# A hybrid S5 and RG-LRU layer on one core: one more product between splits and their users, four S5 runs at once, and a reordered tail

## The chip, the cores and the metric

One core of a Trainium2 chip runs the whole kernel. The metric is device time in microseconds, the median of repeated runs. Engines are named as in the profile: PE is TensorE (matmuls), DVE is VectorE, ACT is ScalarE, POOL is GpSimd, SP is SyncE, which here only issues transfers; POOL issues transfers too.

## The reference, cut to what matters

`x` is 2048 prompt frames and 8 x 16 sample frames of width 1024.

```
h = rmsnorm(x, ln_g);  u_a, z_a, u_b, z_b, g_a, g_b = split(h @ w_in)   # 512 512 1024 1024 1024 1024
y_a = gelu(s5(u_a));  y_a = y_a * sigmoid(y_a @ w_glu + b_glu)
p_a = (y_a * silu(z_a)) @ w_pa
y_b = rglru(conv4(u_b));  p_b = (y_b * silu(z_b)) @ w_pb
m = sigmoid(g_a) * p_a + sigmoid(g_b) * p_b
y = rmsnorm(x + m @ w_out, final_gain)
```

The S5 branch has 32 groups of 16 channels and 64 complex states each, the RG-LRU has 16 heads with block-diagonal gates. The states after the last frame are outputs too. All in float32.

## The kernel before, in words

**Numbers.** Every float32 operand is split into a float16 high part (an ACT copy) and a float16 low part (a DVE subtraction), and a product of two such operands is three passes (high-high, high-low, low-high), the lines 161 to 163 of the listing. A product with 4 blocks of the contracted axis is 12 matmuls of 128x128 by 128x512.

**Tiles.** Time is cut into four prompt tiles of 512 columns (n = 0 to 3) and one sample tile of 128 (n = 4).

**Stages.** (1) For each tile: norm, transposes of `x` into `h`, and the projection `u_a` (`proj`, four products m of 24 matmuls). `trans_tile(n+1, ...)` transposes the next tile behind the products m = 2 and m = 3, four channel blocks behind each; a transpose goes to one of the three buffers of the PSUM tag "a", which ACT and DVE empty (`evac_h`). `norm_sums`, `norm_root` and `norm_scale` for the next tile are written behind the products m = 0 and m = 1. (2) Four column blocks of `g_b` directly. (3) Sixteen pairs of column blocks (`run_pair`), alternating a pair of branch B (`u_b`, `z_b`) and a pair of gates; each pair is two times 7 products (a Strassen-like scheme, 12 matmuls each) and one of the sample tile. (4) The projection of branch B (`wpb`), 5 tiles by 8 blocks; called B below. (5) The tail: for each tile GLU and projection of branch A (`ga_tile`, 4 + 8 products), the output projection and final norm (`out_tile`). In the tail `glu_prep` loads the S5 output `ya` and splits it into `yh`, the first operand of the GLU.

**The order of the work.** All is one program written out in order; each engine runs its own instructions in that order. Beside the products of (2), (3) and (4) generators are advanced by `pump(budget)`, called once behind each product of 12 matmuls (each half product in B, each product of the sample tile): this is a turn. A generator that yields a number or `Step(c)` has put instructions of about c units in the program, and c is taken from the turn's budget; `Step` also ends its part of the turn, and `Later(k)` makes it sit out k turns. The list `tasks` is served first, the list `low` from what is left. In `tasks` are `b_work` (conv, gates and scan of branch B) and, in B, the 16 `s5_run(q)`; in `low` are `w_spill` (44 weight blocks split and stored) and two `s5_prep` (the 16 S5 matrices; the second works only in B).

An `s5_prep` of one q: load parameters, `Later(3)` or in B `Later(6)`, `wb` (five DVE operations, 2.2 units), transposes of `wb` (line 172 on PE, 0.8), `wc` (2.8), matmuls with `wc` (lines 1269 and 1272, 0.9), 0.7, then `kh` is stored to `kpD` and read back shifted as `dd` (0.4). What becomes of `dd`, `lags(q)`, is written during the next q of the same generator: two ACT copies and a store to `sD`; only then is q in `prepared`.

An `s5_run` of one q:

```python
            while q not in prepared or running > 2:
                yield Later(1)
            running += 1
            page = page_b("t1", (2048,), "sp", F32)
```

then it loads `sD[q]` and the inputs, `yield Later(7)`, and has the steps 0.6 (12 matmuls, line 1425), 3.4 (the DVE scan), 0.3, 0.8, 0.6, 0.6, 0.6 (two groups of matmuls, lines 1470 to 1477, whose results are stored to `yDp`). The pages "t1" have four buffers.

Behind B, what is left in the lists is worked off without products, then the tail starts:

```python
        while tasks or low or due:
            beside()
        load_w(wpa, wpaD[1])
```

`gt` tiles come from `slots` buffers, `small` tiles from `NSMALL`. `NO_SPILL` and `NO_PREP` are the turns of two neighbouring pairs (1 to 30) in which `w_spill` and `s5_prep` stand still.

## Time and profile before

| | |
|---|---|
| median of 3 runs | 1581.39 us (1579.0 to 1585.59) |
| the profiled execution | 1582.97 us, its span 1581.2 us |
| PE busy | 1456.8 us (92%), 8168 matmuls |
| DVE, ACT, POOL busy | 1038.7, 813.8, 275.1 us |
| mean granted clock of PE | 0.976 |

The granted clock is 1.0 at 2.4 GHz and 0.5 at 1.2 GHz. Idle time of PE is what a change of the order can win; idle time of another engine costs nothing unless PE waits for it. A matmul of 512 columns starts 0.216 us after the one before it at the full clock, though its own row says 0.38 us, since they overlap: a product of 12 is 2.6 us.

### The profile page before, as it was taken

What the parts mean: (1) busy time and instruction counts of PE and PEld (TensorE: products, weight loads), DVE (VectorE), ACT (ScalarE), POOL (GpSimd) and SP (SyncE); (2) the same over time, 40 slices, a digit from 0 to 9 for tenths busy, and PEclk for the clock granted to TensorE, in tenths of its full rate; (3) what the DMA queues carried; (4) which work ended last, traced back from release to release, by engine and by line L of the source; (5) the groups of instructions that cost most, each with busy time, mean ns of one, the idle gap of its engine ahead of it and who ended that gap; (6) DMA issues with size and microseconds to landing.
All of it is one profiled execution on the core that took longest, in us unless ns stands there. A gap on an engine that the chain in (4) does not pass through costs nothing.

```text
span 1581.2 us, 22662 instructions
## 1 busy us (share of the span) xinstructions
PE 1456.8 (92%) x8168; PEld 727.6 (46%) x8168; DVE 1038.7 (66%) x2137; ACT 813.8 (51%) x1524; POOL 275.1 (17%) x557
## 2 busy tenths in 40 slices
PE   7889999989999999999999999899998789999998
PEld 4444444444444444444444444455556334444444
DVE  5456867858677576877858777456545665757554
ACT  7542335847667575775847576234323432525232
POOL 0680010110201112020111202134324000000000
PEclk9999999999999999999999999999999799999999
DMA  8316222342422334142232408998973914352431
GB/s 203 91 54 247 71 76 78 106 125 70 144 61 96 102 103 134 48 155 64 94 104 77 152 22 296 318 294 287 311 248 105 345 74 148 118 178 89 166 99 69
DMA packets 168490, 222.20 MB, mean 141 GB/s; under 512 B 39259, under 2 KB 117739, under 8 KB 166329
## 3 DMA queue, kind: packets, MB, share of 16 engines
q1 hardware_dynamic: 144440, 150.96, 29.8%
q0 software_dynamic: 23936, 69.79, 12.2%
q8 instruction: 64, 1.05, 0.3%
q14 instruction: 50, 0.40, 0.1%
HBM read 133.85 MB, written 86.84 MB: 140 GB/s over the span
## 4 chain that ended last, share of the span: by engine, by line
PE 55%; DVE 19%; issue 12%; ACT 7%; DMA 4%; POOL 2%; SPq 1%; DVEq 0%; POOLq 0%; ACTq 0%
PE ps_mm L162 14%; PE ps_mm L161 14%; PE ps_mm L163 14%; PE ps_mm L1753 3%; PE ps_mm L1751 3%; PE ps_mm L1752 3%; DVE xc L65 3%; DVE wf L65 2%; DVE yh L53 2%; ACT L74 1%; PE ps_a L1272 1%; ACT pt L74 1%; DVE sz L65 1%; DVE wc L53 1%; DVE q L65 1%
## 5 line engine op out<-in xcount | busy, mean ns | idle before, releaser
L161 PE MATMUL ps_mm<-T,wf 128*128 128x512 f16 x512 | 195.4, 382 | 4.8 <-ACT ub L74 3.7
L163 PE MATMUL ps_mm<-T,wf 128*128 128x512 f16 x512 | 195.4, 382 | 0.5 <-DVE wf L65 0.5
L162 PE MATMUL ps_mm<-T,wf 128*128 128x512 f16 x512 | 195.4, 382 | 0.0
L161 PEld LDWEIGHTS <-wf 128*128 128x128 f16 x1232 | 121.5, 99 | 119.7 <-issue 9.5
L162 PEld LDWEIGHTS <-wf 128*128 128x128 f16 x1232 | 121.5, 99 | 118.6 <-issue 11.7
L163 PEld LDWEIGHTS <-wf 128*128 128x128 f16 x1232 | 121.5, 99 | 118.1 <-issue 5.1
L161 PE MATMUL ps_mm<-h,wf 128*128 128x512 f16 x448 | 173.2, 387 | 2.0 <-ACT wf L74 2.0
L163 PE MATMUL ps_mm<-h,wf 128*128 128x512 f16 x448 | 172.5, 385 | 0.7 <-DVE wf L65 0.7
L162 PE MATMUL ps_mm<-h,wf 128*128 128x512 f16 x448 | 172.9, 386 | 0.0
L1753 PE MATMUL ps_mm<-wo,M 128*128 128x512 f16 (+2 forms) x280 | 104.5, 375 | 5.3 <-DVE M L65 5.3
L1751 PE MATMUL ps_mm<-wo,M 128*128 128x512 f16 (+2 forms) x280 | 104.3, 374 | 0.0
L1752 PE MATMUL ps_mm<-wo,M 128*128 128x512 f16 (+2 forms) x280 | 104.3, 374 | 0.0
L161 PE MATMUL ps_mm<-Y,wpb 128*128 128x512 f16 x256 | 97.8, 382 | 0.4 <-DMA Y<-ybD 0.4
L162 PE MATMUL ps_mm<-Y,wpb 128*128 128x512 f16 x256 | 97.8, 382 | 0.0
L163 PE MATMUL ps_mm<-Y,wpb 128*128 128x512 f16 x256 | 97.6, 381 | 0.0
L65 DVE SCALAR_TENSOR_TENSOR gb<-gb,ps_mm 128x512 f32<-128x512 f32 (+1 forms) x40 | 24.1, 606 | 92.2 <-PE ps_mm L163 74.7
L74 ACT ACT_TABLE_LOAD x62 | 79.5, 1283 | 6.2 <-PE ps_mm L163 4.6
L65 DVE SCALAR_TENSOR_TENSOR xc<-ub,PC,xc 128x512 f32<-128x512 f32 x96 | 71.9, 749 | 2.3
L65 DVE SCALAR_TENSOR_TENSOR xo<-ps_mm,xo 128x512 f32<-128x512 f32 (+2 forms) x35 | 23.7, 676 | 72.5 <-PE ps_mm L1753 72.5
L74 ACT ACTIVATE gs<-ps_mm 128x512 f32<-128x512 f32 (+1 forms) x92 | 48.1, 532 | 44.8 <-PE ps_mm L163 39.3
L65 DVE SCALAR_TENSOR_TENSOR wf<-wraw,wf 128x512 f16<-128x512 f32 (+1 forms) x82 | 55.7, 696 | 12.0 <-ACT wf L74 12.0
L162 PE MATMUL ps_mm<-yA,wt 128*128 128x512 f16 (+1 forms) x160 | 54.2, 347 | 9.8 <-DVE yA L65 9.8
(318 smaller groups left out, 3254.5 us busy)
## 6 DMA issues: line engine op xcount, KB each, us to landing
wraw<-w_in SPq DMA_DIRECT2D x38, 512.0 KB, 4.0
sp<-sD SPq DMA_DIRECT2D x16, 768.0 KB, 7.7
xt<-x_prompt SPq DMA_DIRECT2D x16, 512.0 KB, 4.3
gbD<-gs POOLq DMA_DIRECT2D x32, 256.0 KB, 2.4
ybD<-y POOLq DMA_DIRECT2D x32, 256.0 KB, 3.3
gaD<-gs POOLq DMA_DIRECT2D x32, 256.0 KB, 2.4
Y<-ybD SPq DMA_DIRECT2D x8, 1024.0 KB, 13.8
gb<-gbD SPq DMA_DIRECT2D x32, 256.0 KB, 8.2
```

Of the source, the lines that this page charges most:

```text
L53: V.tensor_tensor(out=out, in0=a, in1=b, op=op)
L65: V.scalar_tensor_tensor(out=out, in0=a, scalar=s, in1=b, op0=op0, op1=op1)
L74: S.activation(out=out, in_=a, func=f, **kw)
L161: PE.matmul(p, lhsT=a[:, 0], rhs=b[:, 0], start=first, stop=False, skip_group_check=more)
L162: PE.matmul(p, lhsT=a[:, 0], rhs=b[:, 1], start=False, stop=False, skip_group_check=more)
L163: PE.matmul(p, lhsT=a[:, 1], rhs=b[:, 0], start=False, stop=last, skip_group_check=more)
L1272: PE.matmul(o[:, 16 + P * j:16 + P * j + w], lhsT=lb, rhs=wc[:, j, g].rearrange("p (h t) -> p t h", t=8)[:, 0:w // 16], start=True, stop=True)
L1751: PE.matmul(p, lhsT=lh[0], rhs=w_[:, 0, c], start=(k == 0), stop=False)
L1752: PE.matmul(p, lhsT=lh[0], rhs=w_[:, 1, c], start=False, stop=False)
L1753: PE.matmul(p, lhsT=lh[1], rhs=w_[:, 0, c], start=False, stop=(k == KB - 1))
```

## The change

- **Transposes.** For tiles 0 to 2 and m = 2, 3 two of the four transposed channel blocks are written in the middle of the product m (behind its fourth block), two behind it.
- **Turns.** `pump` carries what a turn overspent into the next (`debt`, down to -4). The budgets are 2.8 instead of 2.4 in the pairs and 2.5 instead of 2.2 in B.
- **One more product.** `b_work` has an empty stage between `xs_lo` and `gates`; `s5_prep` has a `Later(1)` behind `wb` and one behind `wc`. `kf` and `kh` share a buffer.
- **Windows and buffers.** `NO_SPILL`, `NO_PREP` move; 22 and 9 buffers instead of 21 and 12.
- **S5 runs.** Four at once instead of three, their earliest starts three turns apart instead of four.
- **The start of the tail.** A new task, `tail_start`, waits until all other tasks are done, then loads `wo` (4 x 1 MB) and runs `glu_prep(0)`; this was behind B before.
- **The tail.** Tiles in the order 0, 1, 4, 2, 3; what runs beside which `out_tile` is a table; one more `pump` in each step. Operands of the sample tile are in other buffers.

The diff, cut to its core:

```diff
-        def proj(W, n, tag="mm"):
+        def proj(W, n, tag="mm", between=None):
             p = ps(tag)[:, :TILES[n][1]]
-            gemm(p, W, lambda k: hT(n, k), KB)
+            for k in range(KB):
+                passes(p, W(k), hT(n, k), k == 0, k == KB - 1)
+                if k == 3 and between:
+                    between()
             return p
...
-                    p = proj(lambda k: wua[m][:, k], n)
+                    early = n < 3 and m >= 2
+                    p = proj(lambda k: wua[m][:, k], n,
+                             between=(lambda: trans_tile(n + 1, range(4 * m - 8, 4 * m - 6))) if early else None)
...
-                            trans_tile(n + 1, range(4 * m - 8, 4 * m - 4))
+                            trans_tile(n + 1, range(4 * m - 6, 4 * m - 4))
...
-        NSMALL = 12
-        slots = 21
+        NSMALL = 9
+        slots = 22
...
         def pump(budget):
-            nonlocal turn
+            nonlocal turn, debt
+            budget += debt
...
+            debt = max(-4.0, min(0.0, budget))
...
-            stages = [(taps, 2.0), (xs_hi, 0.1), (xs_lo, 0.7), (gates, 0.4), (input_gate, 0.7), (decay, 0.2),
+            stages = [(taps, 2.0), (xs_hi, 0.1), (xs_lo, 0.7), (lambda n: None, 0), (gates, 0.4), (input_gate, 0.7), (decay, 0.2),
                       (inflow, 0.7)]
...
-        NO_SPILL = range(13, 18)
-        NO_PREP = range(11, 19)
+        NO_SPILL = range(15, 22)
+        NO_PREP = range(13, 22)
...
                 yield Step(2.2)
+                yield Later(1)
                 p = ps("a", (P, 4, P))
...
                 yield Step(2.8)
+                yield Later(1)
                 wcs = gt([P, 2, 2, 2, P], F16, name="wcs")
...
-            run_pair(i, lambda pos, c: tick(2.4 - c))
+            run_pair(i, lambda pos, c: tick(2.8 - c))
...
-            while q not in prepared or running > 2:
+            while q not in prepared or running > 3:
...
-            pump(2.2)
+            pump(2.5)
...
+        def tail_start():
+
+            while len(tasks) > 1 or done["spill"] < 44:
+                yield Later(1)
+            for i in range(4):
+                wo.append(page_load(page_b("t1", (2, 2, D), "wo"), woD[i]))
+                yield Later(1)
+            for _ in glu_prep(0):
+                yield Step(1.4)
+
         for q in range(16):
-            tasks.append([clock + 4 * q, s5_run(q)])
+            tasks.append([clock + 3 * q, s5_run(q)])
+        tasks.append([clock, tail_start()])
...
-        tl = [(n, i) for n in range(NT) for i in range(TILES[n][1] // P)]
+        TAIL = [0, 1, 4, 2, 3]
+        tl = [(n, i) for n in TAIL for i in range(TILES[n][1] // P)]
...
-        for _ in glu_prep(0):
-            pump(0)
         flush()
         ahead = glu_prep(1)
...
-            if i < 4:
-                wo.append(page_load(page_b("t1", (2, 2, D), "wo"), woD[i]))
-            elif i < 6:
-                xload(i - 4)
+            if i < 2:
+                xload(i)
...
-        for n in range(NT):
+        BESIDE = {0: ([1], 2, [4, 2]), 1: ([4, 2], 3, [3]), 4: ([], 0, []), 2: ([3], 2, []), 3: ([], 0, [])}
+        for n in TAIL:
             flush()
-            nxt = ga_tile(n + 1) if n + 1 < NT else iter(())
+            gas, steps, preps = BESIDE[n]
+            nxt = chain(*[ga_tile(x) for x in gas])
+            ahead = chain(*[glu_prep(x) for x in preps])
             for i, _ in enumerate(out_tile(n)):
-                for _ in range(2):
+                pump(0)
+                for _ in range(steps):
+                    next(nxt, None)
                     pump(0)
-                    next(nxt, None)
-                if i == 3 and n + 2 < NT:
-                    ahead = glu_prep(n + 2)
-                if i > 3:
+                if i > 3 or len(preps) > 1:
                     next(ahead, None)
```

## Rows read from the trace of the kernel before

**Rows 1.** Windows by stage: window, length, busy (count) by engine, clock, DMA.
```profile
0.00:137.00 137.00, 113.67 (x627) 62.21 (x627) 71.17 (x175) 71.58 (x142) 63.64 (x182) 0.98 0.46 140
...
258.00:976.00 718.00, 673.43 (x3708) 328.37 (x3706) 534.28 (x990) 482.50 (x841) 105.26 (x195) 0.98 0.32 102
976.00:1216.50 240.50, 228.10 (x1569) 128.26 (x1570) 128.43 (x380) 79.80 (x211) 84.22 (x141) 0.98 0.80 273
1216.50:1243.50 27.00, 11.52 (x73) 6.44 (x72) 16.76 (x35) 13.07 (x23) 7.29 (x13) 0.64 0.65 216
1243.50:1581.20 337.70, 314.39 (x1553) 145.65 (x1550) 200.47 (x409) 118.53 (x223) 1.06 (x2) 0.98 0.38 136
```

**Rows 2.** Waits of PE, window 258:976: us in total, times, longest.
```profile
PE ps_a L162 <- DVE xs L53: 15.0, 9, 2.5
PE ps_a L1272 <- DVE wc L53: 13.0, 6, 3.7
PE ps_a L172 <- DVE wb L53: 11.1, 6, 3.3
```

**Rows 3.** Columns of rows 1: first and last stretch at half clock, pairs.
```profile
490.40:497.30 6.90, 5.83 (x16) 2.66 (x17) 6.13 (x13) 3.77 (x5) 1.53 (x3) 0.51 0.24 85
...
906.90:910.30 3.40, 3.40 (x9) 1.18 (x8) 1.52 (x4) 0.05 (x1) 0.54 (x1) 0.50 0.08 30
```

**Rows 4.** Timeline 26 to 43, stage 1, PE and ACT.
```profile
26.12 0.38 PE L161 MATMUL ps_mm<-h,wua 128*128 128x512 f16 x1
...
35.28 2.19 ACT L74 ACTIVATE xt<-xt,st 128x1024 f32<-128x1024 f32 x2 [0.98 <-DVE st L65]
...
37.35 1.48 PE L172 MATMUL ps_a<-ident,xt 128*128 128x128 f32 x12
...
41.84 0.66 PE L172 MATMUL ps_a<-ident,xt 128*128 128x128 f32 x4 [3.01 <-DVE h L65]
...
42.71 0.39 PE L161 MATMUL ps_mm<-h,wua 128*128 128x512 f16 x1
```

**Rows 5.** Waits of PE in the same stage, window 0:137.
```profile
PE ps_a L172 <- DVE h L65: 12.4, 6, 4.4
```

**Rows 6.** Windows, line 1272 alone (8 for each q): pairs, B.
```profile
258.00:976.00 718.00, 11.34 (x80) 6.78 (x80) 0.98 0.32 102
976.00:1216.50 240.50, 5.67 (x40) 3.43 (x40) 0.98 0.80 273
```

**Rows 7.** Waits of PE, window 976:1216.5 (B).
```profile
PE ps_a L1272 <- DVE wc L53: 5.7, 3, 2.8
...
PE ps_a L172 <- DVE wb L53: 2.0, 2, 1.3
```

**Rows 8.** Timeline behind B, PE: last S5 run, first GLU product.
```profile
1218.05 0.87 PE L1425 MATMUL ps_a<-u,sp 128*128 128x136 f16 x12
...
1242.87 0.63 PE L163 MATMUL ps_mm<-yh,wt 128*128 128x512 f16 x1
```

**Rows 9.** DMA issues, window 976:1240: KB each, median us to landing.
```profile
sp<-sD SPq DMA_DIRECT2D x16, 768.0 KB, 7.7
...
sD<-d POOLq DMA_DIRECT2D x6, 256.0 KB, 6.5
...
dd<-kpD SPq DMA_DIRECT2D x20, 64.0 KB, 3.2
...
kpD<-kh POOLq DMA_DIRECT2D x10, 16.0 KB, 5.8
```

**Rows 10.** Groups by line, ACT, 1010:1240: count, busy, mean ns, idle.
```profile
L74 ACT ACTIVATE d<-dd 128x512 f16<-128x512 f16 x10 | 10.7, 1124 | 0.0
```

**Rows 11.** The page, section 6: issues over the whole span, columns as rows 9.
```profile
wraw<-w_in SPq DMA_DIRECT2D x38, 512.0 KB, 4.0
...
gbD<-gs POOLq DMA_DIRECT2D x32, 256.0 KB, 2.4
```

**Rows 12.** Timeline of PE, tail, tile 2: the longer wait.
```profile
1390.64 0.38 PE L162 MATMUL ps_mm<-yA,wt 128*128 128x512 f16 x1 [1.05 <-DVE yA L65]
```

More of the change, by code (lines that the diff above doesn't have):

```diff
@@ L671, in build @@
         turn = 0
+        debt = 0.0
         def defer(k, f):
@@ L1274, in s5_prep @@
                                   start=True, stop=True)
-                kf, kh = gt([64, 256], name="kf"), gt([64, 2, 256], F16, name="kh")
+                kfh = gt([64, 512], name="kf")
+                kf, kh = kfh[:, 0:256], kfh[:, 256:512].bitcast(F16).rearrange("p (l x) -> p l x", l=2)
                 scopy(kf[:, 16:], pk[0:64, 16:256])
@@ L1342, in build @@
                     lru_states()
-                    low.append([0, w_spill()])
-                    low.extend([0, s5_prep(i)] for i in range(2))
+                    low.extend([0, g] for g in (w_spill(), s5_prep(0), s5_prep(1)))
         next(wg)
@@ L1566, in hook_z @@
             clock += 1
-            pump(2.4 - c)
+            pump(2.8 - c)
             if pos == 7:
@@ L1582, in build, with ya_load, tload, glu_prep @@
         s5_init()
+        def ya_load(m, n):
+            if n < NT - 1:
+                t = gt([P, 8, 2, 32], name="ya")
+                SP.dma_start(out=t.rearrange("p t j c -> p (t j c)"),
+                             in_=yDp[n, 1024 * m:1024 * m + 1024].rearrange("(p t) x -> p (t x)", t=8))
+            else:
+                t = small([P, 8, 2, 8], name="ya")
+                SP.dma_start(out=t.rearrange("p t j c -> p (t j c)"),
+                             in_=yDs[1024 * m:1024 * m + 1024].rearrange("(p t) x -> p (t x)", t=8))
+            return t
+        ya, yh, yA, M = {}, {}, {}, {}
+        def tload(src, m, n, name):
+            t0, w = TILES[n]
+            t = wt(n, name=name)
+            SP.dma_start(out=t, in_=src[m, :, t0:t0 + w])
+            return t
+        def glu_prep(n):
+            w = TILES[n][1]
+            for m in range(4):
+                ya[m, n] = ya_load(m, n)
+            yh[n] = page_a("h", (4, 2, w), "yh") if n < NT - 1 else gt([P, 4, 2, w], F16, "yh")
+            for m in range(4):
+                tv = [yh[n][:, m, l].rearrange("p (c j t) -> p j t c", j=2, t=8) for l in range(2)]
+                yv = ya[m, n].rearrange("p t j c -> p j t c")
+                for j in range(2):
+                    scopy(tv[0][:, j], yv[:, j])
+                def low(tv=tv, yv=yv):
+                    for j in range(2):
+                        tt(tv[1][:, j], yv[:, j], tv[0][:, j], SUB)
+                defer(1, low)
+                yield
+        def tail_start():
[6 more added lines that the diff above has]
+                yield Step(1.4)
         for q in range(16):
-            tasks.append([clock + 4 * q, s5_run(q)])
+            tasks.append([clock + 3 * q, s5_run(q)])
+        tasks.append([clock, tail_start()])
         def load_w(dst, src):
@@ L1630, in build @@
         so2 = out_states2()
-        def ya_load(m, n):
-            if n < NT - 1:
-                t = gt([P, 8, 2, 32], name="ya")
-                SP.dma_start(out=t.rearrange("p t j c -> p (t j c)"),
-                             in_=yDp[n, 1024 * m:1024 * m + 1024].rearrange("(p t) x -> p (t x)", t=8))
-            else:
-                t = small([P, 8, 2, 8], name="ya")
-                SP.dma_start(out=t.rearrange("p t j c -> p (t j c)"),
-                             in_=yDs[1024 * m:1024 * m + 1024].rearrange("(p t) x -> p (t x)", t=8))
-            return t
-        ya, yh, yA, M = {}, {}, {}, {}
-        def tload(src, m, n, name):
-            t0, w = TILES[n]
-            t = wt(n, name=name)
-            SP.dma_start(out=t, in_=src[m, :, t0:t0 + w])
-            return t
-        def glu_prep(n):
-            w = TILES[n][1]
-            for m in range(4):
-                ya[m, n] = ya_load(m, n)
-            yh[n] = page_a("h", (4, 2, w), "yh")
-            for m in range(4):
-                tv = [yh[n][:, m, l].rearrange("p (c j t) -> p j t c", j=2, t=8) for l in range(2)]
-                yv = ya[m, n].rearrange("p t j c -> p j t c")
-                for j in range(2):
-                    scopy(tv[0][:, j], yv[:, j])
-                def low(tv=tv, yv=yv):
-                    for j in range(2):
-                        tt(tv[1][:, j], yv[:, j], tv[0][:, j], SUB)
-                defer(1, low)
-                yield
         def parts(d, t, f):
@@ L1685, in ga_tile @@
             zq = [tload(zaD, m, n, "qz") for m in range(2)]
-            yA[n] = page_a("h", (4, 2, w), "yA")
+            yA[n] = page_a("h", (4, 2, w), "yA") if n < NT - 1 else gt([P, 4, 2, w], F16, "yA")
             for m in range(4):
@@ L1706, in ga_tile @@
                 if m % 4 == 0:
-                    M[n, m // 4] = page_a("h" if m else "h", (4, 2, w), "M")
+                    M[n, m // 4] = page_a("h", (4, 2, w), "M") if n < NT - 1 else hs[:, m:m + 4]
                 p = ps("mm")[:, :w]
@@ L1795, in build @@
                 next(ahead, None)
-        for n in range(NT):
+        BESIDE = {0: ([1], 2, [4, 2]), 1: ([4, 2], 3, [3]), 4: ([], 0, []), 2: ([3], 2, []), 3: ([], 0, [])}
+        for n in TAIL:
             flush()
-            nxt = ga_tile(n + 1) if n + 1 < NT else iter(())
+            gas, steps, preps = BESIDE[n]
+            nxt = chain(*[ga_tile(x) for x in gas])
+            ahead = chain(*[glu_prep(x) for x in preps])
             for i, _ in enumerate(out_tile(n)):
-                for _ in range(2):
+                pump(0)
+                for _ in range(steps):
+                    next(nxt, None)
                     pump(0)
-                    next(nxt, None)
-                if i == 3 and n + 2 < NT:
-                    ahead = glu_prep(n + 2)
-                if i > 3:
+                if i > 3 or len(preps) > 1:
                     next(ahead, None)
             for _ in nxt:
+                pump(0)
+            for _ in ahead:
                 pump(0)
```

## The prediction

> **What bounds the kernel now.** The windows by stage come first [rows 1]: PE is busy for 113.67 us of the first 137, for 673.43 of 718 in the pairs, 228.10 of 240.5 in B, 11.52 of 27 between B and the end of the first GLU product, and 314.39 of 337.7 in the tail. No other engine comes near (DVE in the pairs: 534.28 of 718), so PE and its gaps set the time; the gaps are 44.6 us in the pairs, 23.3 in the first stage, 12.4 in B, 15.5 behind B, 23.3 in the tail. The waits of PE say whose they are: in the pairs 39.1 of the 44.6 us are waits for three DVE results that PE uses one product after they were written, the low part `xs`, `wc` and `wb` [rows 2]; in the first stage 12.4 us are transposes without a free buffer [rows 5]. Then the windows at half clock: in the pairs there are five such stretches, the first from 490.40, 23.9 us in all, and PE is busy for most of each [rows 3]; about 21 us of work, which at full clock would have taken 10.5 less. Each begins in or behind one of those waits. Of 27 us behind B nearly all was at 1.2 GHz (clock 0.64 on average).
>
> The sum is made against the profiled execution (span 1581.2, 1582.97 us in all), which is 1.6 us above the median of the three runs. It is given for the median: 1581.4.
>
> **First stage.** Two channel blocks are transposed half a product (2.6 us) earlier. That frees the third buffer in time, so much of the 12.4 us goes. But the transposes read `xt` scaled, and that isn't ready then: for tile 1 the product m = 2 starts at 26.12, its middle is 28.7, and ACT scales `xt` from 35.28 to 37.47 [rows 4]. The sample products that PE now does between the end of m = 2 (31.3) and 37.35 stand behind the second half and come later. Written out from 37.5: two blocks of transposes 1.0 (12 matmuls take 1.48), half a product 2.6, 72 sample matmuls at a quarter of 0.216 each 4.0, two blocks 1.0 and a short transpose 0.2 end at 46.3, where the next product starts at 42.71 now [rows 4]. So tile 1 loses about 3.5 us; tiles 2 and 3, where the scaling ends a little behind the same place, come out about even. The stall of 9 us may bring half clock behind it, 1 to 3 us. I take +5, between 0 and +9.
>
> **Pairs.** The empty stage and each `Later(1)` put one more product, 2.6 us, between DVE and PE. The nine waits for `xs` (longest 2.5) vanish; of `wc` the two of 3.7 leave 1.1 each, of `wb` three of 3.3 leave 0.7 each [rows 2]: 39.1 becomes 4.3, the rest of the gaps stays. Half clock: 8 of 10.5 us. One prep fewer falls in the pairs (below): 2 us of PE, 1.1 of them line 1272 [rows 6]. Sum -45. The price is on DVE and ACT: a step is only later, none is added, and 534.28 us of DVE work fit in 670 us (80%). The higher budget can't crowd a turn, since overspending is now charged: by the costs in the code the heaviest turn falls from 5.0 to 4.4 units. Bounds: -30 if a third of the waits reappears behind DVE or in the 22 buffers; -53 if no wait of these is left.
>
> **The turns of B.** B has 64 turns of half a product and 8 short ones, 72. The count goes by the yields. Before: three runs of 14 turns each at a time, the sixteenth starts at turn 66 and ends at 79, that is 7 turns behind B; and in the trace the 12 matmuls of run 15 do follow the last product (1218.05, [rows 8]). The preps, too, agree: 10 with one ahead of 258 before B and 5 in it (80 and 40 pieces of 8, [rows 6]).
>
> After: a run costs 6.9 units, a prep 7.8. With the overspending charged, the pairs finish 10 preps, so 6 are left for B. There `tasks` comes first: four runs at once take 4 x 6.9 / 14 = 2.0 of the 2.5 units of a turn, and the two preps live on 0.5, until runs stand still for lack of a prepared q. By the count preps 10 and 11 last from turn 1 to 36, 12 and 13 to 56, 14 and 15 to 71; q = 15 is in `prepared` at turn 77, its run goes from 78 to 91, and `tail_start`, which waits for it, puts the GLU operand at 96 to 100. So 28 turns instead of 8 lie behind the last product, and nothing of the GLU is beside B. Were overspending still forgiven, the same count would end the runs at turn 64 and the operand at 73.
>
> **B itself.** The waits for `wc` and `wb` (7.7 us, [rows 7]) go but for 0.2, its other gaps stay. The mean clock of 0.98 [rows 1] stands for some 10 us at half, 5 us of loss; two thirds go with the waits, 3.4. One more prep costs 2, and two and a half runs move behind the end; a run has 36 matmuls, 12 take 0.87 [rows 8], so 2.6 each, -6.5. Sum -15. More runs and preps compete for buffers and for transfers (the 16 engines are at 0.80 here, [rows 1]): -5 at worst, -17 at best.
>
> **Behind B.** Now run 15 starts its matmuls 1.55 us behind the last product (1216.50), and from there to the end of the first GLU product (1243.5) are 25.45 us [rows 1, 8]. After, run 15 still has a chain ahead of it that nothing covers, one transfer behind the other: `kh` to `kpD` (5.8), `dd` (3.2), two ACT copies of 1.1, the store to `sD` (6.5), the load of `sp` (7.7) [rows 9, 10], 25.4 us, since `kh` is written in the last turn but one of B. Then the same 25.45. The `wo` loads are ahead of `ya` on SP's queue, but three of the four pages are free earlier, and the fourth fits in the wait for `yDp`. So 25.4 - 1.55 = +24, and some 2 us more at half clock: +26. The landings are of a window full of transfers; by quieter rows (2.4 for each of the three small ones, 4.0 for the load, [rows 11]) it is +14. If `wo` does delay `ya`, some 35.
>
> The rows price those four transfers at 23.2 us. The Trainium skill, page "DMA: Bandwidth & Descriptors", section "Anatomy of one DMA", has about 2.0 us and the bytes at 436 GB/s for a transfer that runs alone: as an estimate 2.0, 2.2, 2.6 and 3.8, or 10.6 us, and the whole kernel would be at 1537. The rows of this window differ from it, since their transfers share the engines with others.
>
> **Tail.** The same products in another order. The extra `pump` writes the fourth block's low part of `yA` ahead of the next output product's evacuation; the wait of 1.05 us [rows 12] goes in two tiles. In the step with three products of `ga_tile` a wait of about 2 us appears where two halves of tile 2 meet. The sample tile's own short waits move from the end to a place where they may be longer. I take -2, from -5 to +4.
>
> **Sum.** +5 - 45 - 15 + 26 - 2 = -31: 1581.4 - 31 = 1550.
>
> **Rivals.** *The operand is ready in B, as the words of the change have it.* Then behind B only the first product is left (2.6 instead of 27), some 2 us of half clock go as well, and the runs stay in B (+6.5): -20 instead of +26, so 1504. For it: nothing in the code of `tail_start` keeps it out of B. Against: the count, which does fit the trace of before; it decides at whether q = 15 is prepared by turn 51.
>
> *DVE is what the pairs really wait for.* PE's waits would then be where DVE catches up, and each one removed would come back at the next use: pairs 0 instead of -45, 1595, slower than before. For it: all three waits are for DVE, which in the first stretch of [rows 3] is busy for 6.13 of 6.90 us, and with the chain behind B lengthened only the pairs pay. Against: 74% over the stage. It decides where the pairs save less than 5 us; half as much saved gives 1573.
>
> **How the numbers follow.** My own sum: 0.64, between 1525 and 1572 by the bounds of its parts. The operand ready in B: 0.13. Half the waits of the pairs come back, 1573: 0.11. All: 0.12. No change, for this kernel, is within 0.5%, 1573.5 to 1589.3, about what its runs differ by. Faster 0.64 + 0.13 + half of 0.11 = 0.82, the same 0.07, slower 0.11. The range 1502 to 1583 leaves out the last case and a little below the second.
>
> **What would show it.** Right: in the pairs the waits for `xs`, `wc`, `wb` under 8 us and the stage near 673 us; 48 pieces of line 1272 in B instead of 40; run 15's matmuls some 25 us behind the last product of B, and the first GLU product's end some 50 behind it at half clock; in the first stage a new wait of 8 to 9 us for `xt` in the middle of a product. Wrong: GLU products directly behind B (then the count of turns failed), or PE waits in the pairs of another name that add up to 20 us and more.

## The result, and the profile after

The changed kernel takes 1572.2 us (median of 8 runs, 1566.9 to 1577.6) against 1581.8 for the kernel before (8 runs): ratio 0.9933, 95% interval 0.9907 to 0.9959. It is faster by 9.6 us where 31 were forecast. The execution that was profiled, whose stages are shown here, took 1577.57 us (span 1575.8), the longest of the eight; a second profile of the same kernel (f2, below) took 1570.07.

By stage, with the borders at the same products of both kernels (first product, first of the direct stage, first of the pairs, first and last of B, last matmul of the first GLU product). First the kernel before, then the changed one; the columns are window, length, PE busy (count), clock, DMA share, GB/s:

```profile
14.75:138.31 123.56, 107.53 (x594) 0.97 0.41 125
138.31:234.16 95.85, 93.05 (x497) 0.98 0.31 101
234.16:982.93 748.77, 701.63 (x3879) 0.98 0.33 104
982.93:1216.46 233.53, 222.50 (x1547) 0.99 0.80 270
1216.46:1243.50 27.04, 11.56 (x73) 0.64 0.65 215
1243.50:1581.20 337.70, 314.39 (x1553) 0.98 0.38 136
```

```profile
15.48:147.47 131.99, 112.18 (x594) 0.90 0.39 115
147.47:248.03 100.56, 96.12 (x496) 0.95 0.29 96
248.03:948.24 700.21, 685.55 (x3848) 1.00 0.33 109
948.24:1176.31 228.07, 221.30 (x1508) 0.99 0.77 265
1176.31:1233.35 57.04, 22.41 (x146) 0.60 0.69 235
1233.35:1575.80 342.45, 318.17 (x1553) 0.96 0.35 124
```

The pairs give 48.6 us and B 5.5. All of the other four stages take some back: 8.4, 4.7, 30.0 and 4.8. In the first, the second and the last the number of matmuls is the same within a record or two, yet PE is busy 4.7, 3.1 and 3.8 us longer: the same work, more of it at half clock.

**Pairs.** The waits of PE in 248.03:948.24 (us in total, times, longest; of before, [rows 2]):

```profile
PE ps_mm L161 <- ACT ub L74: 8.1, 5, 4.7
PE ps_mm L161 <- ACT gs L74: 2.0, 2, 1.4
PE ps_mm L161 <- DVE zb L53: 1.5, 2, 1.2
PE ps_a L162 <- DVE xs L53: 1.2, 1, 1.2
PE ps_mm L163 <- DVE wf L65: 1.0, 1, 1.0
PE ps_a L161 <- ACT pt L74: 0.9, 2, 0.7
```

`wb` and `wc` are gone, `xs` has 1.2 left. New is the wait for `ub`. Its longest, in the timeline of ACT and PE:

```profile
533.20 0.63 ACT L74 ACTIVATE wq<-wr 128x512 f16<-128x512 f32 x1 [8.15 <-DMA wr<-w_pb]
...
534.88 0.60 ACT L74 ACTIVATE ub<-ps_mm 128x512 f32<-128x512 f32 x1
...
535.52 0.59 PE L161 MATMUL ps_mm<-T,wf 128*128 128x512 f16 x1 [4.65 <-ACT ub L74]
```

ACT stands 8.15 us at a step of `w_spill` whose load hasn't landed, and the evacuation of a product is queued behind it. The chain is load, ACT, buffer, PE; the row of PE names only its last link.

**First stage.** Timeline of ACT and PE, and the stretches at half clock (windows, columns as above):

```profile
37.09 2.19 ACT L74 ACTIVATE xt<-xt,st 128x1024 f32<-128x1024 f32 x2 [0.98 <-DVE st L65]
...
37.90 0.87 PE L172 MATMUL ps_a<-ident,xt 128*128 128x128 f32 x2 [8.29 <-DVE xt L69]
```

```profile
33.90:44.10 10.20, 5.91 (x18) 0.52 0.31 50
74.80:81.60 6.80, 6.32 (x19) 0.52 0.18 41
91.90:98.70 6.80, 5.03 (x15) 0.52 0.50 184
112.40:115.80 3.40, 3.40 (x12) 0.55 0.02 5
```

The forecast stall of 8 to 9 us in the middle of a product is there, 8.29. The waits for `xt` add up to 13.2 us, and 4.3 are left of those for a free buffer, which had 12.4 [rows 5]; 27 us of the stage run at half clock.

**Behind B.** Timeline of DVE, PE and ACT (of before, [rows 8]), then DMA landings in 1150:1233 (KB, median us; of before, [rows 9]):

```profile
1180.52 0.29 DVE L65 SCALAR_TENSOR_TENSOR gb<-gb,ps_mm 128x128 f32<-128x128 f32 x1 [4.56 <-DMA gb<-gbD]
1184.38 0.28 DVE L65 SCALAR_TENSOR_TENSOR gb<-gb,ps_mm 128x128 f32<-128x128 f32 x1
1184.58 0.41 DVE L65 SCALAR_TENSOR_TENSOR kf<-kf 64x256 f16<-64x256 f32 x1
...
1203.31 1.52 PE L1435 MATMUL ps_a<-u,sp 128*128 128x136 f16 x12 [3.54 <-DMA u<-uD]
...
1222.15 4.50 ACT L74 ACTIVATE yh<-ya 128x256 f16<-128x256 f32 x4 [6.06 <-DMA ya<-yDp]
...
1224.55 0.59 PE L161 MATMUL ps_mm<-yh,wt 128*128 128x512 f16 x1 [8.95 <-ACT yh L74]
```

```profile
sp<-sD SPq DMA_DIRECT2D x4, 768.0 KB, 5.0
...
sD<-d POOLq DMA_DIRECT2D x4, 256.0 KB, 2.3
...
dd<-kpD SPq DMA_DIRECT2D x8, 64.0 KB, 3.0
...
kpD<-kf POOLq DMA_DIRECT2D x4, 16.0 KB, 3.4
```

Run 15's matmuls come 27.0 us behind the last product, and the first GLU product ends 30.0 later. No GLU product is beside B. The landings above are medians of all transfers in the window. Run 15's own, from the issue to the landing of the one that ended last, took 2.3 us (store to `kpD`), 2.2 (`dd`), 2.3 (store of `d`) and 5.0 (its inputs: `u`, issued right behind `sp`).

**B.** Waits of PE, first 982.93:1216.46 of the kernel before, then 948.24:1176.31 of the changed one, and the windows of B's own matmuls alone (`wpb`; busy PE, clock, DMA share, GB/s), in the same order:

```profile
PE ps_a L1470 <- ACT v L74: 4.8, 1, 4.8
PE ps_a L1272 <- DVE wc L53: 3.7, 2, 2.8
PE ps_a L172 <- DVE wb L53: 2.0, 2, 1.3
```

```profile
PE ps_a L1486 <- ACT hst L74: 3.9, 1, 3.9
PE ps_a L1282 <- DVE wc L53: 2.6, 1, 2.6
```

```profile
982.93:1216.46 233.53, 185.29 (x960) 0.99 0.80 270
948.24:1176.31 228.07, 185.27 (x960) 0.99 0.77 265
```

**Tail.** Timeline of PE, the two longest new waits, in the sample tile and where the step of three products joins the halves of tile 2:

```profile
1366.08 0.27 PE L162 MATMUL ps_mm<-yA,wt 128*128 128x128 f16 x1 [2.24 <-DVE yA L65]
...
1410.20 0.58 PE L162 MATMUL ps_mm<-yA,wt 128*128 128x512 f16 x1 [3.91 <-DVE st L53]
```

### The profile page after: what moved, and what is told of

It reads as the page before. It is cut to its first block, busy times and chain, and to the rows that moved or that the text cites. A ratio compares the mean times of both kernels' runs of the same rounds, so it can differ in the third digit from the quotient of the medians.

```text
span 1575.8 us, 22665 instructions
## 1 busy us (share of the span) xinstructions
PE 1462.2 (93%) x8168; PEld 735.3 (47%) x8168; DVE 1039.9 (66%) x2137; ACT 816.1 (52%) x1524; POOL 275.3 (17%) x557
## 3 DMA queue, kind: packets, MB, share of 16 engines
q8 instruction: 64, 1.05, 0.3%
## 4 chain that ended last, share of the span: by engine, by line
PE 71%; DVE 9%; ACT 6%; DMA 6%; issue 5%; SPq 1%; POOL 1%; DVEq 0%; ACTq 0%; POOLq 0%
PE ps_mm L161 18%; PE ps_mm L162 18%; PE ps_mm L163 18%; PE ps_mm L1775 3%; PE ps_mm L1773 3%; PE ps_mm L1774 3%; DMA wraw<-w_in 1%; PE ps_a L172 1%; ACT L74 1%; DVE yh L53 1%; PE ps_a L1282 1%; DVE xc L65 1%; PE ps_a L162 1%; PE ps_a L161 1%; PE ps_a L163 1%
## 5 line engine op out<-in xcount | busy, mean ns | idle before, releaser
L162 PEld LDWEIGHTS <-wf 128*128 128x128 f16 x1232 | 120.8, 98 | 124.7 <-issue 15.7
L161 PE MATMUL ps_mm<-h,wf 128*128 128x512 f16 x448 | 170.6, 381 | 2.0 <-ACT wf L74 2.0
L163 PE MATMUL ps_mm<-h,wf 128*128 128x512 f16 x448 | 170.4, 380 | 0.7 <-DVE wf L65 0.7
L162 PE MATMUL ps_mm<-h,wf 128*128 128x512 f16 x448 | 170.5, 381 | 0.0
L1775 PE MATMUL ps_mm<-wo,M 128*128 128x512 f16 (+2 forms) x264 | 99.2, 377 | 5.3 <-DVE M L65 5.3
L1773 PE MATMUL ps_mm<-wo,M 128*128 128x512 f16 (+2 forms) x264 | 99.1, 377 | 0.0
L1774 PE MATMUL ps_mm<-wo,M 128*128 128x512 f16 (+2 forms) x264 | 99.0, 376 | 0.0
```

What stands on the lines that cost most here:

```text
L161: PE.matmul(p, lhsT=a[:, 0], rhs=b[:, 0], start=first, stop=False, skip_group_check=more)
L162: PE.matmul(p, lhsT=a[:, 0], rhs=b[:, 1], start=False, stop=False, skip_group_check=more)
L163: PE.matmul(p, lhsT=a[:, 1], rhs=b[:, 0], start=False, stop=last, skip_group_check=more)
L1773: PE.matmul(p, lhsT=lh[0], rhs=w_[:, 0, c], start=(k == 0), stop=False)
L1774: PE.matmul(p, lhsT=lh[0], rhs=w_[:, 1, c], start=False, stop=False)
L1775: PE.matmul(p, lhsT=lh[1], rhs=w_[:, 0, c], start=False, stop=(k == KB - 1))
```

## Experiments

All have the ratio to runs of the kernel before on the same chip. Stages in us, from the windows of each kernel's profile with the borders above; "turns" is the count, from the code, of turns behind B until the work that B should cover is done (the runs; with `tail_start` the GLU operand too). The expectations of g2, h2 and h3 put f1's stage behind B at 11 us and g4's at 12; between the borders named above it is 9.2 and 10.4.

| kernel | median | ratio (95%) | first | direct | pairs | B | turns | behind B | tail |
|---|---|---|---|---|---|---|---|---|---|
| before | 1581.8 | 1 | 123.6 | 95.9 | 748.8 | 233.5 | 8 | 27.0 | 337.7 |
| changed | 1572.2 | 0.9933 (0.9907 to 0.9959) | 132.0 | 100.6 | 700.2 | 228.1 | 28 | 57.0 | 342.5 |
| f2, changed again | 1568.2 | 0.9908 (0.987 to 0.9946) | 124.7 | 100.5 | 700.0 | 228.7 | 28 | 56.6 | 342.6 |
| e1 | 1524.6 | 0.9647 (0.9623 to 0.9672) | 121.4 | 98.9 | 700.1 | 232.7 | 1 | 9.2 | 343.9 |
| f3 | 1647.6 | 1.0422 (1.0376 to 1.0468) | 117.8 | 97.9 | 711.7 | 256.9 | 62 | 105.4 | 337.8 |
| h3 | 1529.1 | 0.9658 (0.9626 to 0.969) | 122.9 | 99.3 | 700.7 | 235.6 | 14 | 25.0 | 329.2 |
| e4 | 1548.0 | 0.9782 (0.9765 to 0.9799) | 123.9 | 95.7 | 688.3 | 232.7 | 15 | 51.1 | 339.8 |
| g1 | 1567.2 | 0.9903 (0.9877 to 0.993) | 122.2 | 96.1 | 768.4 | 222.9 | 1 | 9.5 | 330.8 |
| g2 | 1525.3 | 0.9636 (0.961 to 0.9662) | 118.3 | 97.3 | 685.6 | 230.1 | 23 | 46.0 | 328.8 |
| e2 | 1562.2 | 0.9881 (0.9864 to 0.9897) | 118.0 | 97.9 | 699.3 | 228.9 | 28 | 57.4 | 342.2 |
| f4 | 1589.9 | 1.0047 (1.0025 to 1.007) | 131.3 | 97.3 | 750.2 | 234.8 | 8 | 27.0 | 338.4 |
| e3 | 1556.2 | 0.9851 (0.9826 to 0.9876) | 127.5 | 97.9 | 700.1 | 228.6 | 28 | 56.3 | 330.2 |
| h1 | 1573.9 | 0.9944 (0.9923 to 0.9966) | 122.6 | 96.1 | 749.7 | 235.4 | 8 | 27.1 | 329.7 |
| g3 | 1518.4 | 0.9586 (0.9562 to 0.961) | 118.2 | 97.4 | 699.9 | 236.8 | 1 | 10.3 | 340.3 |
| f1 | 1509.6 | 0.9547 (0.9519 to 0.9575) | 121.7 | 98.4 | 702.6 | 230.9 | 1 | 9.2 | 330.8 |
| g4 | 1506.8 | 0.9513 (0.9487 to 0.9538) | 116.4 | 101.3 | 700.4 | 233.4 | 1 | 10.4 | 329.9 |
| h2 | 1495.9 | 0.9454 (0.9436 to 0.9473) | 118.8 | 96.1 | 700.0 | 229.8 | 0 | 5.1 | 329.1 |

**e1, no charge for overspending** (from the changed kernel):

```diff
         def pump(budget):
             nonlocal turn, debt
-            budget += debt
```

> The changed kernel, except that overspending of a turn's budget is forgiven as in the kernel before; all else stays. Theory (the charge starves the preps, and that alone keeps the GLU operand out of B): the operand is written one turn behind B, so the 57 us from the last product of B to the end of the first GLU product become 3 to 10; B takes back the matmuls of two and a half runs, +6; the pairs keep their 704. Sum about -43, near 1529. Rival 1 (the charge is what emptied the pairs' waits, not the extra product): the pairs go back towards 735, and the total is 1560 or more. Rival 2 (the chain of transfers of run 15 sets the end, whatever the turns): 45 us and more stay behind B, and the total stays within 10 us of 1572.

As expected: the stage behind B falls from 57.0 to 9.2, B takes 4.6 back, the pairs keep their 700. Its window behind B, columns as above:

```profile
1168.18:1177.41 9.23, 4.43 (x14) 0.79 0.91 288
```

Both rivals fall: the pairs don't need the charge, and the chain of transfers is no floor where it starts early enough.

**f3, the charge alone** (from the kernel before):

```diff
+        debt = 0.0
...
-            nonlocal turn
+            nonlocal turn, debt
+            budget += debt
...
+            debt = max(-4.0, min(0.0, budget))
```

> The kernel before with one edit alone: overspending is charged to the next turns, at its old budgets of 2.4 and 2.2. Theory (the charge starves the preps): by the count of turns the work of B ends 62 turns behind its last product, not 8; at 1.5 us a turn (8 turns took 27 us, 28 took 57) 27 us become about 105, the pairs stay near 745 to 750 and keep their waits for xs, wc and wb; total +60 to +80, near 1650. Rival (the charge evens out DVE's turns, and that is what emptied the waits): the pairs come under 720, and the total below 1600.

The total (1647.6) and the stage behind B (105.4) came as the count had them. The pairs didn't: 711.7 instead of 745 to 750. Line 1275 alone (eight pieces for each prep) in the windows pairs, B and behind B:

```profile
230.37:942.11 711.74, 6.73 (x48) 0.99 0.27 90
942.11:1199.04 256.93, 10.19 (x72) 0.92 0.76 253
1199.04:1304.47 105.43, 1.12 (x8) 0.57 0.61 202
```

6 preps fall in the pairs where 12 did, 9 in B, one behind it. With half the preps, two fifths of the gaps go too: 47.1 us become 28.5, those for `wc` and `wb` 6.8 where [rows 2] has 24.1 in its shorter window. So the charge emptied some waits, by putting work off to where it costs more. The rival had the pairs right and the total wrong.

**h3, the charge in the pairs alone** (from f1, below):

```diff
             nonlocal turn, debt
+            if branch_b:
+                budget += debt
```

> The kernel of f1 with overspending charged in the pairs, and forgiven in B. By the count 10 preps instead of 12 fall in the pairs, and the GLU operand is written 14 turns behind B: with the charge in both places it is 28, without it 1. Theory (both places bite, each for about half): from 11 us behind B to 35 to 48, pairs as in f1 or 2 less, total +22 to +35, near 1538. Rival (only the charge in B bites, since there the runs take two units of each turn's 2.5 ahead of the preps): behind B stays under 20 us, total within 6 us of f1.

Between the two: 25.0 behind B, under the 35 to 48 expected, and +19 in all by the medians; 14 turns were priced too high. The charge in the pairs costs 16 us behind B (9.2 to 25.0) and 5 in B, where two preps more are left; the one in B costs the other 32 behind it (25.0 to 57.0 in the changed kernel). Both bite, that in B harder.

**e4, the product more alone** (from the kernel before):

```diff
-            stages = [(taps, 2.0), (xs_hi, 0.1), (xs_lo, 0.7), (gates, 0.4), (input_gate, 0.7), (decay, 0.2),
+            stages = [(taps, 2.0), (xs_hi, 0.1), (xs_lo, 0.7), (lambda n: None, 0), (gates, 0.4), (input_gate, 0.7), (decay, 0.2),
...
                 yield Step(2.2)
+                yield Later(1)
...
                 yield Step(2.8)
+                yield Later(1)
```

> The kernel before with one edit alone, the product more between splits and users: the empty stage of the branch's pipeline and one turn behind each of wb and wc. Theory: the pairs go from 754 to about 706, as in the changed kernel, since this edit alone empties the waits for xs, wb and wc; by the count of turns run 15 ends 15 turns behind B instead of 7, so 27 us there become 35 to 45; first stage, direct stage and tail as before. Total -30 to -40, near 1547. Rival 1 (DVE is what the pairs wait for, and the charge is what relieved it): the pairs stay above 735. Rival 2 (a later step needs more buffers than there are, 21 here): waits under other names, pairs 720 to 735.

The one edit takes 60.5 us from the pairs, more than was expected and more than the whole change does, and the total is 24 us under the changed kernel. Behind B it takes 51.1 us, not 35 to 45: DVE stands 8.77 us there at a `gb` that hasn't landed (until 1162.75), ahead of the runs' scans, which the count of turns doesn't know. All waits of PE in its pairs:

```profile
PE ps_a L1274 <- DVE wc L53: 5.1, 3, 1.9
PE ps_mm L163 <- DVE wf L65: 1.0, 1, 1.0
```

Nothing for ACT here, and 9 preps in the stage instead of 10.

**g1, without that product** (from f1):

```diff
-            stages = [(taps, 2.0), (xs_hi, 0.1), (xs_lo, 0.7), (lambda n: None, 0), (gates, 0.4), (input_gate, 0.7), (decay, 0.2),
+            stages = [(taps, 2.0), (xs_hi, 0.1), (xs_lo, 0.7), (gates, 0.4), (input_gate, 0.7), (decay, 0.2),
...
                 yield Step(2.2)
-                yield Later(1)
...
                 yield Step(2.8)
-                yield Later(1)
...
-            lags(*dd)
+            if dd:
+                lags(*dd)
```

> The kernel of f1 (the changed kernel with overspending forgiven, the old transposes and the old order of the tail) without the product more between splits and users: no empty stage, no turn behind wb and wc. Theory (that product alone empties the pairs' waits): they come back, 10 to 16 us each for xs, wc and wb, the pairs go from 703 to 740 to 755, B and what is behind it stay at 230 and 11; total +40 to +50, near 1553. Rival (the charge run alone cut the pairs to 712, so it is how DVE's turns are filled that matters): pairs under 725, total under 1530.

The pairs go to 768.4 and the total to +58, both above the range expected; all 16 preps now fall in the pairs (12 in f1). Waits of PE in the pairs:

```profile
PE ps_a L1279 <- DVE wc L53: 28.2, 8, 4.0
PE ps_a L162 <- DVE xs L53: 14.8, 16, 1.7
PE ps_a L172 <- DVE wb L53: 6.1, 9, 2.7
```

The three old names come back with 49.1 us. The rival falls.

**g2, the old budget in the pairs** (from f1):

```diff
-            run_pair(i, lambda pos, c: tick(2.8 - c))
+            run_pair(i, lambda pos, c: tick(2.4 - c))
...
-            pump(2.8 - c)
+            pump(2.4 - c)
```

> The kernel of f1 with the pairs' budget back at 2.4 (2.5 in B stays). Theory: waits for ACT (gs, ub: 8.6 us) thin out and 9 or 10 preps instead of 12 fall in the pairs, so these go from 703 to 688 to 692, as in the run with the product alone; but by the count of turns the GLU operand is written 23 turns behind B instead of one, and 11 us there become 45 to 55. Total +25 to +32, near 1538. Rival (B's budget is enough by itself to catch up): behind B under 25, total 1510 or less.

46.0 us behind B and pairs without a wait for ACT, as expected; these gain 17 rather than 11 to 15 (8 preps there instead of 12): 7.3 of PE's work and 9.7 of its gaps. So the total is +16 and not +25 to +32. The larger budget buys an operand that is ready one turn behind B for 17 us of the pairs.

**e2, late transposes** (from the changed kernel):

```diff
-                    early = n < 3 and m >= 2
+                    early = False
...
-                            trans_tile(n + 1, range(4 * m - 6, 4 * m - 4))
+                            trans_tile(n + 1, range(4 * m - 8, 4 * m - 4))
```

> The changed kernel with the transposes back where they were, four channel blocks behind each of the products m = 2 and m = 3. Theory (the early half reads what ACT hasn't scaled yet, and each stall brings half clock): the waits of 8.3, 4.3, 3.1 us go, the first stage goes from 147.5 to 138, the direct stage stays at 95, total -9, near 1563. Rival (the half-clock stretches of the first stage come from its short bursts, wherever the transposes stand): the stage stays above 144 and the total within 4 us.

1562.2: first stage 118.0, direct stage 97.9, the rest as it was. By the ratios 8.2 us come back against the changed kernel's first runs, 4.3 against f2's.

**f4, early transposes alone** (from the kernel before, with `proj` as in the changed one):

```diff
-                    p = proj(lambda k: wua[m][:, k], n)
+                    early = n < 3 and m >= 2
+                    p = proj(lambda k: wua[m][:, k], n,
+                             between=(lambda: trans_tile(n + 1, range(4 * m - 8, 4 * m - 6))) if early else None)
...
-                            trans_tile(n + 1, range(4 * m - 8, 4 * m - 4))
+                            trans_tile(n + 1, range(4 * m - 6, 4 * m - 4))
```

> The kernel before with one edit alone: two of the four channel blocks transposed in the middle of the products m = 2 and m = 3 of the first stage. Theory: a stall of 8 us in tile 1 and half clock behind it, against 12.4 us of waits for a free buffer that go: first stage +3 to +9, total +5 to +8, near 1588. Rival 1 (it is neutral, and the 9 us in the profile were chance): within 2 us of 1581. Rival 2 (it saves what it was to save): 1575 or less.

**f2, the changed kernel once more:**

> The changed kernel again, as a yardstick on the same chip as the other runs of this batch: 1567 to 1578. Theory (half clock in the first stage comes by chance of the execution, more often behind the early transposes): its first stage, from the first product to the first of the direct stage, was 132 us in the profile shown and 121 and 127.5 in two kernels with the same first stage; here anything from 120 to 133. Rival (132 us is what this stage always takes): 131 to 133.

Alone the early transposes cost 7.4 us (0.0025 to 0.007 of 1582, 4 to 11). One profile tells this stage badly. f2's first stage:

```profile
15.19:139.89 124.70, 107.83 (x595) 0.95 0.40 123
```

7.3 us less than the first profile of the very same kernel, 4.4 of them in PE's busy time. Over the five profiles with early transposes (121.4 to 132.0) the mean is 127.4, over the ten with the old ones (117.8 to 123.9) 120.9: +6.5. The direct stage is +1.9 by the same means, with overlap (97.3 to 100.6 against 95.7 to 99.3). It differs as much between kernels whose program is the same up to its end: 101.3 in g4 and 96.1 in h2. There PE's wait for `dTe` is 4.3 us and 2.2 long, and behind the first one 6.8 us run at half clock, behind the second none. The changed kernel has 3.8 us of it in both profiles (before 2.1) and 6.8 us at half clock behind it; e3, with the same program, has 3.8 and 3.4. Whether the change makes the longer wait more frequent stays open.

**g4, early transposes for m = 3 alone** (from f1):

```diff
-                    early = False
+                    early = n < 3 and m == 3
...
-                            trans_tile(n + 1, range(4 * m - 8, 4 * m - 4))
+                            trans_tile(n + 1, range(4 * m - (6 if early else 8), 4 * m - 4))
```

> The kernel of f1 with two channel blocks transposed early in the product m = 3 alone, where ACT has scaled the tile by then. Theory: the waits for a free buffer behind m = 3 (2.0, 0.9 and 0.9 us) go, no wait for xt appears in the middle of m = 3, and half clock stays as it is: first stage -2 to -5, total -2 to -5, near 1506. Rival (any transpose in the middle of a product brings half clock, wherever its data stand): first stage 124 to 130, total +3 to +8.

1506.8, 3 us under f1, with intervals that overlap. Its first stage (116.4, and 118.8 in h2, which has it too) lies at the low end of the ten with the old transposes. A gain isn't settled, but the rival falls: in these two profiles the waits for `xt` add up to 0.7 and 1.0 us, and a transpose in the middle of a product does no harm where its data are ready.

**e3, the old order of the tail** (from the changed kernel):

```diff
-        TAIL = [0, 1, 4, 2, 3]
+        TAIL = list(range(NT))
...
-        BESIDE = {0: ([1], 2, [4, 2]), 1: ([4, 2], 3, [3]), 4: ([], 0, []), 2: ([3], 2, []), 3: ([], 0, [])}
+        BESIDE = {0: ([1], 2, [2]), 1: ([2], 2, [3]), 2: ([3], 2, [4]), 3: ([4], 2, []), 4: ([], 0, [])}
```

> The changed kernel with the tiles of the tail in the order 0, 1, 2, 3, 4 and two steps of the next tile's GLU behind each output product; the rest of the tail's edits stay (one more turn of deferred work for each product, the sample tile's own buffers). Theory (the waits of 2.2 and 3.9 us and the two half-clock stretches at 1365 and 1409 belong to the sample tile in the middle): the tail goes from 342.5 to 336 to 338, total -5. Rival (the tail's new waits come from the extra turn of deferred work): the tail stays at 342, and the total within 2 us.

The tail falls by 12.3, more than twice what was expected, to below the kernel before. Of these 4.9 are PE's busy time (318.17 to 313.25 for the same matmuls, at half clock for longer) and the rest waits.

**h1, the third turn alone** (from the kernel before):

```diff
             for i, _ in enumerate(out_tile(n)):
+                pump(0)
                 for _ in range(2):
-                    pump(0)
                     next(nxt, None)
+                    pump(0)
```

> The kernel before with one edit alone: the deferred work is pumped once ahead of and once behind each of the two GLU steps beside an output product (three turns instead of two). Theory (this alone is the tail's gain seen with the old order): the waits for yA and yh (11.3 us) fall to about 4, the tail goes from 337.7 to 330 to 331, total -6 to -8, near 1575. Rival (the sample tile's own buffers or the earlier loads of the next operand gave it): the tail stays within 2 us of 337.7.

As expected, 329.7. Waits of PE in its tail (before: `yA` 9.8 in 14 times, `M` 5.3, `yh` 1.5):

```profile
PE ps_mm L1753 <- DVE M L65: 5.6, 3, 2.1
PE ps_mm L162 <- DVE yA L65: 3.8, 7, 1.8
```

So the tail's edits were one of -8.0 and one of +12.3.

**g3, sample tile third, two steps** (from f1):

```diff
-        TAIL = list(range(NT))
+        TAIL = [0, 1, 4, 2, 3]
...
+        BESIDE = {0: ([1], 2, [4, 2]), 1: ([4, 2], 2, [3]), 4: ([], 0, []), 2: ([3], 2, []), 3: ([], 0, [])}
```

> The kernel of f1 with the sample tile third again, but with two steps of the GLU beside each output product of tile 1 instead of three. Theory (the wait of 3.9 us in tile 2 is that of the step of three, those of 2.2 and 0.5 us are the sample tile's short products, and each brings 6.8 us of half clock): the tail goes from 330 to 334 to 337, total +4 to +7 on f1. Rival 1 (the order is harmless with two steps): within 2 us of f1. Rival 2 (all of the 12 us are the sample tile's): the tail at 341 to 343.

Tail 340.3: it gives back 9.5 of 12, outside what theory and the first rival had, and near the second. It doesn't settle how the 12 divide: with two steps eight GLU products of tile 2 stand in a row with no output product between them and wait for `yA` up to 2.76 us, which is a stall of its own. Any way of putting the sample tile third that was tried here loses.

**f1, three parts undone together** (the edits of e1, e2 and e3, from the changed kernel):

```diff
-            budget += debt
...
-                    early = n < 3 and m >= 2
+                    early = False
...
-        TAIL = [0, 1, 4, 2, 3]
+        TAIL = list(range(NT))
...
```

> The changed kernel with three of its parts undone together: overspending forgiven, four channel blocks of transposes behind each product again, tiles of the tail in the order 0 to 4. Theory (the three are independent): 1572 - 48 - 10 - 16 as measured one by one gives 1498; by stages 118 to 124 for the first, 96, 700, 231, 11 behind B and 330 in the tail, with 15 ahead of the first product, 1501 to 1507. Rival (the gains overlap, since half clock falls on whichever stall is left): 1515 or more.

1509.6: 12 above the sum of the single effects, 3 above the range by stages, and under the rival's 1515. Every stage is as in the single runs. Four S5 runs at once, their closer starts, the moved windows, the buffers and `tail_start` are in all kernels made from the changed one; no run has them alone, so what each of them is worth stays open.

**h2, a bigger budget beside B** (from g4):

```diff
         def beside():
...
-            pump(2.5)
+            pump(3.5)
```

> The kernel of g4 with the budget of a turn beside B at 3.5 instead of 2.5. Theory: by the count the GLU operand is written in the last turn of B instead of one behind it, so 12 us from the last product of B to the end of the first GLU product become 4 to 8; more work per turn lets PE wait in B, 0 to +3. Total -2 to -6, near 1503. Rival (what is left behind B is the landing of ya, 5 us and more, that no turn can hasten): within 2 us of 1507.

Behind B 5.1 us, and that at full clock:

```profile
1159.73:1164.78 5.05, 2.91 (x13) 1.00 1.04 408
```

1495.9 us, 0.9454 of the kernel before and the fastest of all: 76 us under the changed kernel with six lines of it different. That is 11 under g4 where 2 to 6 were expected. Behind B 5.3 went, and B, where PE was expected to wait longer, is 3.6 shorter; in the profiles the direct stage is 5.2 shorter too, which this edit doesn't touch.

## Why the prediction was right and wrong

The direction held, and so did the mechanism in the pairs and behind B; the size was a third. The steps that failed are the terms B and the tail: they miss by 9.5 and 6.8 us, and by 10.1 and 6.9 in f2, nearly all of the 18.0 us that f2's sum misses. By stages, forecast and measured (first profile; f2):

| term | forecast | measured | f2 |
|---|---|---|---|
| ahead of the first product | 0 | +0.7 | +0.4 |
| first stage | +5 (0 to +9) | +8.4 | +1.1 |
| direct stage | 0 | +4.7 | +4.7 |
| pairs | -45 (-53 to -30) | -48.6 | -48.8 |
| B | -15 (-17 to -5) | -5.5 | -4.9 |
| behind B | +26 (+14 to +35) | +30.0 | +29.6 |
| tail | -2 (-5 to +4) | +4.8 | +4.9 |
| sum | -31 | -5.5 | -13.0 |

**The count of turns** was the best part. It put the operand 28 turns behind B and not beside it, 62 turns for f3, one for e1, and each time the stage behind B was about as long as expected. But turns have no fixed price: 14 gave 25.0 us (h3) and 15 gave 51.1 (e4), where nearly the same was expected. The 48 pieces of line 1272 (1282 now) in B are there: 6 preps. For the kernel before the count was one off: the window from 976 starts 7 us ahead of B's first product, and between the right borders 12 preps fall in the pairs and 4 in B, not 11 and 5. The rival "operand ready in B", at 0.13, is not what the changed kernel does; e1 comes near it, with 47.8 us less behind B where the rival had 46.

**Behind B** (+26, measured +30) came out near by two errors that cancel, which is luck. "`kh` is written in the last turn but one of B" failed: its low part is written from 1184.58 to 1185.0 (as `kf`, since both share a buffer now), 8.7 us behind the last product. DVE, which works in order, stands 4.56 us at a `gb` that hasn't landed, and has 3.6 us of a run to do ahead of the next one. Run 15's four transfers then took 2.3, 2.2, 2.3 and 5.0 us, 11.7 instead of 23.2, in a stage with the DMA engines at 0.69 and not at 0.80. The two copies took about what was counted, 2.1, and some 4.5 lie between the links: in issues that queue, and in ACT, which stands at the end of an earlier run's scan before it gets to the copies. Late start, gaps and faster transfers give 27.0 where 25.4 stood. The Trainium skill, page "DMA: Bandwidth & Descriptors", section "Anatomy of one DMA", had given 10.6 as an estimate for the transfers, from a fit for those that GpSimd issues (two of these four are SP's): nearer to these 11.7 than the rows of the loaded window were. The stretch from run 15's matmuls on took 30.0 instead of 25.45. The 4.6 us more lie ahead of the GLU product, which itself takes 8.8 in both kernels: run 14's second step now stands between run 15's two (9.5 us from the first to the second instead of 7.2), and from there to the GLU product it is 11.7 instead of 9.4.

**Pairs** (-45, measured -48.6): gaps of PE give 32.5 where 34.8 were counted, and its busy time 16.1 where 10 were, with two preps fewer in the stage instead of one. But two opposite effects hide in it. The product more is worth 60.5 by itself (e4), and 65.8 between g1 and f1. "The higher budget can't crowd a turn, since overspending is now charged" failed: with 2.8 the stage has waits for ACT, a spill step ahead of its load among them, and more preps, together 17 us in the one pair of kernels that differs in this alone (g2 and f1). The charge prevents none of this: the pairs are 700 with it and without. The rival that DVE is what the pairs wait for is refuted for the waits left (of 14.7 us ACT has 11.0), but not without a grain: f3 shows that fewer preps on DVE make fewer waits.

**B** (-15, measured -5.5) is the term most wrong. PE's gaps fall by 4.3 us and not 7.5: 2.6 of the waits for `wc` stay, the 4.8 for `v` go, but 3.9 for `hst` come, and 2 us of the old ones lay ahead of B's first product, so that they count in the pairs. That "two thirds go with the waits, 3.4" of half clock failed outright: between the borders B had two stretches of 3.4 us at half clock (from 1026.3 and 1080.9) and has two again (from 989.3 and 1170.2), and its own 960 matmuls keep PE busy for 185.3 us in both kernels. Counting each matmul up to the start of the next, two preps more cost 2.8 (2 for one was counted), and the matmuls of the two runs that moved behind B give 5.0 (6.5 was counted, for two and a half).

**Tail** (-2, measured +4.8, beyond its bound): "the wait of 1.05 us goes in two tiles" was too little, the third turn is worth 8.0 (h1); "a wait of about 2 us" for the new order was far too little, it costs 12.3 (e3): 7.3 of PE's gaps and 4.9 of its busy time, at half clock.

**First and direct stage** (+5 and 0, measured +8.4 and +4.7; +1.1 and +4.7 in f2): the stall was foreseen to the microsecond (8.3), but not what follows it. In tile 1 the next product was written out to start at 46.3, and starts at 49.87, of which 0.7 is the later start of the stage: the early transposes take 2.6 us instead of 1.0, and the half product behind them 4.2 instead of 2.6, most of it at half clock. Over many profiles the first stage is +6.5. The direct stage had no term at all; its +4.7 is a longer wait and half clock behind it, which comes and goes between executions.

The errors of the pairs and behind B cancel, those of the first and direct stage add 8.1 us in the first profile and 0.8 in f2, and B and the tail are left. Half clock is a good part of the sum's error: for the same matmuls PE is busy 4.7, 3.1 and 3.8 us longer in the first stage, the direct stage and the tail (0.3, 3.1 and 3.6 in f2), and the 3.4 us that B was to give back didn't come. For each stall removed its half clock was counted, for those added hardly any. And the bounds were treated as independent, though B ended at its unfavourable bound and the tail beyond its own.

## What to carry to other kernels

Where helpers share a budget of turns, simulate the turns: the end of the slowest chain followed from the count alone, and a rule that looks like mere bookkeeping (overspending charged) cost some 45 us, while the edit worth most gave 60 in its stage. Book half clock behind every stall that an edit makes just as behind those that it removes, and look at a stage in several executions before a difference of 5 us is laid to an edit. When a change has many parts, run each alone: here one gave 60, one 8, three took back 45, 12 and 7, and the version with the good parts and a larger budget beside B is 5.5% faster than the kernel before.

## What the runs showed of the hardware

- The first stage of one and the same kernel took 132.0 us in one execution and 124.7 in another, with 594 and 595 matmuls that kept PE busy for 112.18 and 107.83 us: 27 us at 1.2 GHz in the one, and a clock of 0.95 instead of 0.90 over the stage in the other. Their waits for `xt` and `h` add up to 17.5 and 14.6 us.
- Behind B, where PE waits five times for 3.5 to 10 us, most of its work runs at 1.2 GHz: the clock averaged 0.60 over the 57.0 us there (PE busy for 22.4) and 0.57 over 105.4 us in f3; with only 5.1 us there (h2) it never fell.
- Kernels with the same program up to the end of the direct stage had one wait there of 2.2 us and no half clock behind it, or of 4.3 us and 6.8 us of half clock (h2 and g4).
- A wait of PE for ACT can be a late load: 4.65 us for `ub` at 535.52 were 8.15 us of ACT for the landing of `wr`.
